# Summing the second layer's adaLN vectors on VectorE in pieces of 512 columns, from the first mixer on

## The chip, the core and the metric

The kernel runs on one core of a Trainium2 chip. Its engines are TensorE (PE, matrix products into PSUM), VectorE (DVE), ScalarE (ACT), GpSimd (POOL) and SyncE (SP, which issues most of the DMAs). The metric is the device time of one execution in microseconds (us), the median over runs. "Span" is the time from the first to the last instruction of the one execution that the profiler recorded.

## What is computed

Two layers over 256 tokens of width 2048. Each layer has a mixer and a channel mixer (ffn), each behind an RMSNorm that is modulated by vectors of an adaptive layer norm (adaLN), and each added back through a gate vector. The reference, cut to that:

```python
for layer in range(2):
    sh1, sc1, g1, sh2, sc2, g2 = split(silu(c) @ ada_w[layer] + ada_b[layer], 6)   # 6 vectors of 2048
    hn = rms_norm(h, norm_g[layer, 0]) * (1 + sc1) + sh1
    mix = even_mixer(hn, ...) if layer == 0 else chunk_mlp_mixer(hn, ...)
    h = h + g1 * mix
    hn2 = rms_norm(h, norm_g[layer, 1]) * (1 + sc2) + sh2
    h = h + g2 * conv_ffn(hn2, ...)
out = rms_norm(h, final_g)
```

`even_mixer` is a gated 31-tap convolution beside a state-space layer (S5), which also needs a projection of 256 context tokens; `chunk_mlp_mixer` (the odd mixer) is a gated MLP with a 128x128 mixing of tokens. Each adaLN vector (l, v) takes a matrix of 2048 x 2048 in f32, 16.8 MB, for one row of products. The six vectors of layer 1 together read about 100 MB.

## The kernel before

**Products.** Weights come in slabs of 128 x 2048 f32 (1 MB, tile `raw`, four buffers, `RAW`), by SP. A slab has two halves of 1024 columns; a half is split into `hi` (ScalarE, L129) and `lo` = raw - hi (L132, on VectorE, or on GpSimd for every `pool_every`-th half), three buffers each. A half feeds 12 matmuls of 512 columns: two token halves, two rows of the half, and three products each (L136 to L138: hi with xh, lo with xh, hi with xl). One half is called a half-step below. `groups` runs half-steps for one column group of a weight matrix, and after each of them gives some credit to queues of side work: `pump` (S5, convolution, LayerNorm pieces), `cpump`, and `ada_pump`.

**adaLN vectors.** `ada_q[0]` makes the vectors (0,2) to (0,5) on TensorE: a slab of `ada_w` in a `raw` buffer and four matmuls against `cst` (L199). `ada_q[1]` makes the six of layer 1 on VectorE, in the order (1,1), (1,0), (1,2), (1,4), (1,3), (1,5): for each of the 16 rows of slabs two slabs of 128 x 1024 (512 KB, tile `rawa`, two buffers in the pool `yp`), each with one product `acc = raw * cst[:, kt] + acc` (L241) into `adacc`, 128 x 2048. The bias row is loaded into partition 0 of a cleared `adacc` (a memset on GpSimd, L229, and a DMA, L230). At the end `fin` sums over the partitions with four matmuls of `ones` against `adacc`, side by side on 32 columns of the array each (L248), copies on ScalarE, and transposes on TensorE (vectors 0, 1, 3, 4) or writes a row to DRAM (`gate_out`, gates 2 and 5).

**Credits.** `ada_pump(n, k)` adds n credits to queue k and issues items while there is credit. A pair such as `(0.3, 0.48)` in `ADA_F0` gives queue 0 and queue 1 their credits for one slab, half of it after each half-step. Before, an item of queue 1 (one product of 1024 columns) costs 0.5. `ADA_F0` and `ADA_F1` belong to the ffn of layer 0 and 1 (first and second half of the input projection; output projection), `ADA_O1`, `ADA_O2` to the odd mixer's two projections. Before, queue 1 gets nothing in the even mixer. `ada_until` issues what is left of a vector when its consumer comes (`mod_vecs`, `gate_row`).

**Order.** The stages of the profiled execution, by time: the even mixer's first column groups up to 192 us; group 6 (24 matmuls a half-step, since the context is projected too) 192 to 260; groups 4 and 5, the S5 layer, the convolution and its LayerNorm 260 to 391; the even output projection 391 to 578; ffn of layer 0 578 to 1219 (input projection groups 629 to 799 and 896 to 1102, output projection 799 to 896 and 1102 to 1219); odd mixer 1219 to 1545; ffn of layer 1 1545 to 2118 in the same order (1603 to 1747 input, 1747 to 1846 output, 1846 to 2026 input, 2026 to 2118 output); final norm to 2130. The framework orders instructions on each engine by program order, with `high_priority` moving some ahead; each engine then works through its own queue in order.

Of the kernel before, what the change touches and what calls it, by code (L numbers as in the profile page):

```python
# [8 lines left out]
F32 = mybir.dt.float32  # L9
# [6 lines left out]
D = 2048  # L16
# [12 lines left out]
RC = {0: 3.0, 6: 2.5, 4: 2.5, 5: 2.5}  # L29
RS = {4: 2.0, 5: 2.0, 7: 0.4, 8: 2.2}  # L30
# [20 lines left out]
ADA_F0 = [((0.3, 0.48), (0.0, 0.44)), (0.0, 1.0)]  # L51
ADA_B = (0, 4, 0)
ADA_O1 = (0.0, 0.8)
ADA_O2 = (0.0, 0.7)
ADA_F1 = [((0.0, 0.54), (0.0, 0.5)), (0.0, 0.0)]
# [3 lines left out]
class Builder:  # L59
# [121 lines left out]
    def ada_setup(self, pe, dve):  # L181
        self.ada_q = [[i for lv in pe for i in self.ada_items(*lv)], [i for lv in dve for i in self.ada_items_v(*lv)]]
        self.ada_v = dve
        self.ada_credit = [0.0, 0.0]
        self.ada_T = {}
        self.ada_row = {}
# [35 lines left out]
    def ada_items_v(self, l, v):  # L222

        nc = self.nc
        st = {}

        def open_():
            acc = st["acc"] = self.yp.tile([128, D], F32, name="adacc", tag="adacc", bufs=1)
            nc.gpsimd.memset(acc, 0.0)  # L229
            nc.sync.dma_start(acc[0:1], self.A["ada_r"][l, v])  # L230

        def slab(i):
            kt, c = i // 2, slice(1024 * (i % 2), 1024 * (i % 2) + 1024)

            def f():
                if i == 0:
                    open_()
# [6 lines left out]
        def fin():  # L244
            acc = st["acc"]
            ps = self.ms_bank()
            for j in range(4):
                nc.tensor.matmul(ps[32 * j:32 * j + 32, :], self.ones[:, :32], acc[:, 512 * j:512 * j + 512],  # L248
                                 start=True, stop=True, tile_position=(0, 32 * j))
            x = self.small("wk", [128, 512], bufs=4)  # L250
            nc.scalar.activation(x, ps, AF.Copy)
            if v in (2, 5):
                self.gate_out(l, v, x)
                return
            tp = self.tp_bank()
            for b in range(4):
                nc.tensor.transpose(tp[:, 128 * b:128 * b + 128], x[:, 128 * b:128 * b + 128], self.ident)
            t = self.cp.tile([128, 1, 16], F32, name=f"adaT{l}{v}")
            nc.vector.tensor_copy(t[:, 0].rearrange("p (j b) -> p j b", j=4),
                                  tp.rearrange("p (b j r) -> p j b r", b=4, j=4)[:, :, :, 0])  # L260
            self.ada_T[l, v] = t

        return [(0.5, slab(k)) for k in range(2 * KT)] + [(0.5, lambda: None), (0.0, fin)]
# [166 lines left out]
    def setup(self):  # L430
# [6 lines left out]
        sil = self.small("sil", [128, 2, 16], bufs=1)  # L437
# [402 lines left out]
    def conv_setup(self, p):  # L840
# [6 lines left out]
        self.cvT = p.tile([32, 3 * NB + 128], F32, name="cvT")  # L847
# [5 lines left out]
    def conv31(self, m, z):  # L853
# [37 lines left out]
        def inv():  # L891
            ps = self.ms_bank()
            for b in range(2):
# [3 lines left out]
                nc.tensor.matmul(o, self.cvT[:, 3 * NB:], st["t"], start=False, stop=True)  # L897
# [6 lines left out]
    def even(self):  # L904
# [104 lines left out]
        for m in ORDER:  # L1009
            if m != 6:  # L1010
                gate(m, self.groups(W, [m], tok, q4, (ADA_E[m], 0.0), rate=RS[m], crate=RC[m])[m])
# [9 lines left out]
            ps = self.groups(W, [6], toks, [(q, 0) for q in range(4)], (ADA_E[6], 0.0), rate=0.0, crate=RC[6], width=4)[6]  # L1021
# [26 lines left out]
        while self.cv:  # L1048
            self.cpump(2.0)
            self.pump(RS[7])  # L1050
            self.ada_pump(ADA_C)
        mh, ml = self.mh, self.ml = self.xpair()
        for f in self.ln_items():
            f()
            self.pump(RS[7])
            self.ada_pump(ADA_C)
# [376 lines left out]
```

## Time and profile before

| | us |
|---|---|
| median of 3 runs | 2126.47 (2126.03 to 2138.9) |
| the profiled execution | 2132.22 |
| its span | 2130.4 |
| TensorE busy | 1969.8 |
| VectorE busy | 1589.1 |
| ScalarE busy | 963.5 |
| GpSimd busy | 770.1 |
| VectorE: products of the adaLN vectors (L241), 192 of them | 337.6 |

The profiler's views used here: the page of the whole execution; a table of busy time by stretch (also for one source line alone); groups of instructions by line; waits by who waited for whom; a timeline; DMA issues. Busy time of TensorE overlaps between neighbouring matmuls, so its share does not tell whether it runs at its peak; the length of a stretch that does the same work as another does.

### The profile page before, as it was taken

What the parts mean: (1) busy time and instruction counts of PE and PEld (TensorE: products, weight loads), DVE (VectorE), ACT (ScalarE), POOL (GpSimd) and SP (SyncE); (2) the same over time, 40 slices, a digit from 0 to 9 for tenths busy, and PEclk for the clock granted to TensorE, in tenths of its full rate; (3) what the DMA queues carried; (4) which work ended last, traced back from release to release, by engine and by line L of the source; (5) the groups of instructions that cost most, each with busy time, mean ns of one, the idle gap of its engine ahead of it and who ended that gap; (6) DMA issues with size and microseconds to landing.
All of it is one profiled execution on the core that took longest, in us unless ns stands there. A gap on an engine that the chain in (4) does not pass through costs nothing.

```text
span 2130.4 us, 25758 instructions
## 1 busy us (share of the span) xinstructions
PE 1969.8 (92%) x9412; PEld 1493.6 (70%) x9412; DVE 1589.1 (75%) x2535; ACT 963.5 (45%) x1323; POOL 770.1 (36%) x379
## 2 busy tenths in 40 slices
PE   5999999999799979999989799999899989999997
PEld 2566676667477747777777577777678867888886
DVE  5466376665679994879999776866778997368874
ACT  3354253743455433344444353343455544355553
POOL 4311143011034424444434244444434443444443
PEclk8999999999899999999999999999999999999999
DMA  9983553866886877876667778777766566555562
GB/s 375 401 345 109 185 193 142 328 262 219 305 306 225 295 299 254 294 269 230 217 243 267 266 271 292 251 254 274 273 230 215 198 242 238 182 191 185 183 203 108
DMA packets 91931, 522.90 MB, mean 245 GB/s; under 512 B 11318, under 2 KB 11750, under 8 KB 42262
## 3 DMA queue, kind: packets, MB, share of 16 engines
q1 hardware_dynamic: 88684, 517.09, 66.9%
q10 hardware_dynamic: 2736, 3.01, 0.4%
q8 instruction: 74, 1.21, 0.2%
q0 software_dynamic: 384, 1.16, 0.1%
q14 instruction: 53, 0.43, 0.1%
HBM read 519.09 MB, written 2.13 MB: 245 GB/s over the span
## 4 chain that ended last, share of the span: by engine, by line
PE 27%; DVE 15%; DMA 5%; issue 3%; ACT 1%; POOL 1%; ACTq 0%; SPq 0%; DVEq 0%; POOLq 0%
PE mm L137 9%; PE mm L138 9%; PE mm L136 8%; DVE adacc L241 5%; DMA rawa<-in_ada_w 5%; DVE lo L132 4%; DVE ca L1225 2%; DVE cg L1225 1%; POOL lo L132 1%; PE tp L1209 1%; ACT hi L129 0%; DVE al L1277 0%; DVE xl L399 0%; DMA lnrow<-in_o_ln 0%; DVE ca L1275 0%
## 5 line engine op out<-in xcount | busy, mean ns | idle before, releaser
L132 POOL TENSOR_TENSOR lo<-raw,hi 128x1024 fp32r<-128x1024 f32 x253 | 668.1, 2641 | 1208.5 <-ACT hi L129 1144.3
L129 ACT ACTIVATE hi<-raw 128x1024 fp32r<-128x1024 f32 x568 | 598.4, 1059 | 833.0 <-PE mm L138 659.0
L137 PE MATMUL mm<-lo,xh 128*128 128x512 f32 x1632 | 653.2, 400 | 44.8 <-DVE lo L132 44.7
L136 PE MATMUL mm<-hi,xh 128*128 128x512 f32 x1632 | 659.0, 405 | 0.9 <-ACT hi L129 0.6
L138 PE MATMUL mm<-hi,xl 128*128 128x512 f32 x1632 | 646.9, 397 | 1.7 <-DVE xl L399 1.2
L132 DVE TENSOR_TENSOR lo<-raw,hi 128x1024 fp32r<-128x1024 f32 x315 | 432.2, 1375 | 207.6 <-ACT hi L129 207.1
L241 DVE SCALAR_TENSOR_TENSOR adacc<-rawa,cst,adacc 128x1024 f32<-128x1024 f32 x192 | 337.6, 1766 | 92.2 <-DMA rawa<-in_ada_w 88.9
L137 PEld LDWEIGHTS mm<-lo,xh 128*128 128x128 f32 x1632 | 313.3, 192 | 120.2 <-DVE lo L132 58.8
L136 PEld LDWEIGHTS mm<-hi,xh 128*128 128x128 f32 x1632 | 311.7, 192 | 109.2 <-issue 31.1
L138 PEld LDWEIGHTS mm<-hi,xl 128*128 128x128 f32 x1632 | 312.6, 192 | 69.8 <-DVE xl L399 1.8
L137 PE MATMUL mm<-lo,ah 128*128 128x512 f32 x640 | 258.6, 404 | 12.4 <-DVE lo L132 11.6
L136 PE MATMUL mm<-hi,ah 128*128 128x512 f32 x640 | 257.5, 403 | 2.4 <-ACT hi L129 2.4
L138 PE MATMUL mm<-hi,al 128*128 128x512 f32 x640 | 257.1, 402 | 0.0
L1225 DVE SCALAR_TENSOR_TENSOR cg<-tp,fcw,cg 128x189 f32<-128x189 f32 (+2 forms) x512 | 180.7, 420 | 9.9 <-ACT cg L1212 9.9
L1225 DVE SCALAR_TENSOR_TENSOR ca<-tp,fcw,ca 128x189 f32<-128x189 f32 (+2 forms) x512 | 180.5, 419 | 9.7 <-ACT ca L1212 9.7
L137 PEld LDWEIGHTS mm<-lo,ah 128*128 128x128 f32 x640 | 122.7, 192 | 48.4 <-DVE lo L132 16.2
L136 PEld LDWEIGHTS mm<-hi,ah 128*128 128x128 f32 x640 | 122.3, 191 | 34.6 <-ACT hi L129 4.2
L138 PEld LDWEIGHTS mm<-hi,al 128*128 128x128 f32 x640 | 122.4, 191 | 30.6 <-issue 1.7
L199 PE MATMUL ad<-raw,cst 128*32 128x512 f32 x512 | 79.4, 614 | 6.9 <-DMA raw<-in_ada_w 6.9
L407 DVE TENSOR_TENSOR wk<-mm,grow 128x512 f32<-128x512 f32 x56 | 38.0, 684 | 27.8 <-PE mm L138 27.7
L408 DVE TENSOR_TENSOR h<-h,wk 128x512 f32<-128x512 f32 x56 | 56.8, 1022 | 1.2
L387 PE MATMUL tp<-ident,wk 128*128 128x128 f32 x160 | 28.3, 308 | 22.0 <-DVE wk L373 10.8
(273 smaller groups left out, 1462.8 us busy)
## 6 DMA issues: line engine op xcount, KB each, us to landing
raw<-in_f_w_in SPq DMA_DIRECT2D x128, 1024.0 KB, 4.9
rawa<-in_ada_w SPq DMA_DIRECT2D x192, 512.0 KB, 5.8
raw<-in_ada_w SPq DMA_DIRECT2D x84, 1024.0 KB, 5.2
raw<-in_f_w_out SPq DMA_DIRECT2D x64, 1024.0 KB, 4.9
raw<-in_o_w_in SPq DMA_DIRECT2D x32, 1024.0 KB, 5.3
raw<-in_e_w_in SPq DMA_DIRECT2D x28, 1024.0 KB, 6.7
raw<-in_e_w_out SPq DMA_DIRECT2D x16, 1024.0 KB, 5.2
raw<-in_o_w_out SPq DMA_DIRECT2D x16, 1024.0 KB, 5.4
```

Source lines behind the costliest of these rows:

```text
L129: nc.scalar.activation(hi, raw, AF.Copy)
L132: eng.tensor_sub(lo, raw, hi.bitcast(F32))
L136: nc.tensor.matmul(ps, xh, wh, start=first, stop=False)
L137: nc.tensor.matmul(ps, xh, wl, start=False, stop=False)
L138: nc.tensor.matmul(ps, xl, wh, start=False, stop=last)
L199: nc.tensor.matmul(st["ps"][32 * j:32 * j + 32, :], self.cst[:, kt], raw[:, 512 * j:512 * j + 512], start=kt == 0, stop=kt == KT - 1, tile ...
L241: nc.vector.scalar_tensor_tensor(a, raw, self.cst[:, kt, 0:1], a, op0=OP.mult, op1=OP.add)
L387: self.nc.tensor.transpose(tp[:, a * 256 + t * 128:a * 256 + t * 128 + 128], z[t][:, c0:c0 + 128], self.ident)
L407: nc.vector.tensor_mul(m, ps[t], row[:, c])
L408: nc.vector.tensor_add(h[:, t, c], h[:, t, c], m)
L1209: nc.tensor.transpose(tp[:, a * 256 + t * 128:a * 256 + t * 128 + 128], z[t][:, c0 + 128 * a:c0 + 128 * a + 128], self.ident)
L1225: nc.vector.scalar_tensor_tensor(oo, s[:, y0 + dy:y1 + dy, x0 + dx:x1 + dx], w, oo, op0=OP.mult, op1=OP.add)
```

## The change

The products of queue 1 are made for 512 columns at a time, and the queue gets credit from the first mixer on.

- A vector is four blocks j of 512 columns. A block clears an accumulator `adc` of 128 x 512 (in the pool `sp`, one buffer), loads its bias row, and then takes four slabs q of 1 MB from a re-laid-out copy `ada_x`, each with four products of 128 x 512. A product costs 0.25 credits, a slab and `fin` cost none.
- In the even mixer a slab lies in one of the weights' four `raw` buffers; from layer 0's ffn on (`self.late`) in `rawa`, two buffers of 1 MB.
- `fin(j)`: for shift and scale vectors four matmuls with 128 columns of `adc` as stationary operand against two columns of `ones`, and a copy of four columns on VectorE; for gates one matmul, a copy of 32 partitions on ScalarE, and a DMA of one row. It stands right behind the last product of its block.
- Credits: `ADA_V` is new for the even mixer, the credits of the two ffn and the odd mixer's input projection are lower.
- To make room: `sil` takes a `modr` buffer, and the convolution's bias row moves from the last row of `e_conv_w` to the first, so that the bias product uses one row of `ones` and `cvT` loses 128 columns.

```diff
+ADA_V = {6: 1.5, 4: 1.2, 5: 1.2, 7: 0.6, 8: 1.2, 9: 1.2}
-ADA_F0 = [((0.3, 0.48), (0.0, 0.44)), (0.0, 1.0)]
+ADA_F0 = [((0.3, 0.22), (0.0, 0.22)), (0.0, 0.8)]
-ADA_O1 = (0.0, 0.8)
+ADA_O1 = (0.0, 0.5)
 ADA_O2 = (0.0, 0.7)
-ADA_F1 = [((0.0, 0.54), (0.0, 0.5)), (0.0, 0.0)]
+ADA_F1 = [((0.0, 0.3), (0.0, 0.3)), (0.0, 0.0)]
...
     def ada_items_v(self, l, v):
...
-                raw = self.yp.tile([128, 1024], F32, name="rawa", tag="rawa", bufs=2)
-                nc.sync.dma_start(raw, self.A["ada_w"][l, v, kt, :, c])
-                a = st["acc"][:, c]
-                nc.vector.scalar_tensor_tensor(a, raw, self.cst[:, kt, 0:1], a, op0=OP.mult, op1=OP.add)
+        def slab(j, q):
+            def f():
+                if q == 0:
+                    st["acc"] = self.small("adc", [128, 512], bufs=1)
+                    nc.gpsimd.memset(st["acc"], 0.0)
+                    nc.sync.dma_start(st["acc"][0:1], self.A["ada_r"][l, v, :, 512 * j:512 * j + 512])
+                if self.late:
+                    raw = self.yp.tile([128, 4, 512], F32, name="rawa", tag="rawa", bufs=2)
+                else:
+                    raw = self.wp.tile([128, 2048], F32, name="raw", tag="raw", bufs=RAW)
+                    raw = raw.rearrange("p (k n) -> p k n", k=4)
+                nc.sync.dma_start(raw, self.A["ada_x"][l, v, j, q])
+                st["raw"] = raw
+            return f
+        def prod(j, q, k):
+            def f():
+                a = st["acc"]
+                kt = 4 * q + k
+                nc.vector.scalar_tensor_tensor(a, st["raw"][:, k], self.cst[:, kt, 0:1], a, op0=OP.mult, op1=OP.add)
+            return f
+        def fin(j):
+            def f():
+                acc = st["acc"]
+                ps = self.ms_bank()
+                if v in (2, 5):
+                    nc.tensor.matmul(ps[:32], self.ones[:, :32], acc, start=True, stop=True)
+                    x = self.small("wk", [128, 512], bufs=4)
+                    nc.scalar.activation(x[:32], ps[:32], AF.Copy)
+                    if j == 0:
+                        st["d"] = self.dp.tile([4, 512], F32, name="rowd", tag="rowd")
+                    nc.sync.dma_start(st["d"][j:j + 1], x[0:1])
+                    if j == 3:
+                        self.ada_row[l, v] = st["d"]
+                    return
+                for b in range(4):
+                    nc.tensor.matmul(ps[:, 2 * b:2 * b + 2], acc[:, 128 * b:128 * b + 128], self.ones[:, :2],
+                                     start=True, stop=True)
...
-        return [(0.5, slab(k)) for k in range(2 * KT)] + [(0.5, lambda: None), (0.0, fin)]
+        out = []
+        for j in range(4):
+            for q in range(4):
+                out.append((0.0, slab(j, q)))
+                out += [(0.25, prod(j, q, k)) for k in range(4)]
+            out += [(0.0, fin(j))]
+        return out
...
-                gate(m, self.groups(W, [m], tok, q4, (ADA_E[m], 0.0), rate=RS[m], crate=RC[m])[m])
+                gate(m, self.groups(W, [m], tok, q4, (ADA_E[m], ADA_V[m]), rate=RS[m], crate=RC[m])[m])
...
-            ps = self.groups(W, [6], toks, [(q, 0) for q in range(4)], (ADA_E[6], 0.0), rate=0.0, crate=RC[6], width=4)[6]
+            ps = self.groups(W, [6], toks, [(q, 0) for q in range(4)], (ADA_E[6], ADA_V[6]), rate=0.0, crate=RC[6], width=4)[6]
...
             self.ada_pump(ADA_C)
+            self.ada_pump(ADA_V[7], 1)
...
-        self.out_proj(WO, h, row, mh, ml, q4[:3], None, (ADA_EO, 0.0), rate=RS[8])
+        self.out_proj(WO, h, row, mh, ml, q4[:3], None, (ADA_EO, ADA_V[8]), rate=RS[8])
...
-        self.out_proj(WO, h, row, mh, ml, q4[3:], ssq, (ADA_EO, 0.0))
+        self.out_proj(WO, h, row, mh, ml, q4[3:], ssq, (ADA_EO, ADA_V[9]))
```

## Rows read from the trace of the kernel before

**Rows 1.** The page: busy time by engine; DMA rate in 40 slices of the span.

```profile
PE 1969.8 (92%) x9412; PEld 1493.6 (70%) x9412; DVE 1589.1 (75%) x2535; ACT 963.5 (45%) x1323; POOL 770.1 (36%) x379
...
GB/s 375 401 345 109 185 193 142 328 262 219 305 306 225 295 299 254 294 269 230 217 243 267 266 271 292 251 254 274 273 230 215 198 242 238 182 191 185 183 203 108
```

**Rows 2.** Stretches: length; busy PE, PEld, DVE, ACT, POOL; clock, DMA share, GB/s.

```profile
260.00:391.00 131.00, 125.30 (x921) 84.55 (x918) 88.21 (x158) 67.43 (x123) 46.22 (x56) 0.96 0.54 200
...
391.00:553.00 162.00, 154.28 (x964) 110.19 (x964) 104.35 (x175) 74.76 (x121) 16.87 (x7) 0.96 0.72 268
...
192.00:578.00 386.00, 359.63 (x2264) 246.34 (x2263) 236.25 (x417) 173.85 (x296) 70.95 (x66) 0.95 0.62 230
...
629.00:751.00 122.00, 121.46 (x574) 94.81 (x574) 115.09 (x218) 65.41 (x85) 54.39 (x21) 1.00 0.72 264
...
799.00:896.00 97.00, 94.25 (x392) 74.09 (x393) 59.90 (x50) 36.81 (x37) 45.86 (x18) 0.97 0.77 270
...
896.00:1102.00 206.00, 190.39 (x838) 152.86 (x837) 190.64 (x293) 95.20 (x120) 91.29 (x34) 0.98 0.68 242
...
1603.00:1747.00 144.00, 138.42 (x635) 113.09 (x634) 138.76 (x263) 78.19 (x101) 62.64 (x25) 1.00 0.60 213
...
1747.00:1846.00 99.00, 95.14 (x402) 74.36 (x401) 64.27 (x83) 39.26 (x42) 40.40 (x17) 0.98 0.61 217
...
1846.00:2026.00 180.00, 180.00 (x823) 149.11 (x822) 134.35 (x268) 95.68 (x119) 76.28 (x33) 1.00 0.54 187
...
2026.00:2118.00 92.00, 91.54 (x395) 73.18 (x393) 56.66 (x78) 40.81 (x52) 38.65 (x16) 1.00 0.44 149
```

**Rows 3.** The same stretches, line L241 alone: length, busy DVE, clock, DMA, GB/s.

```profile
629.00:751.00 122.00, 19.05 (x10) 1.00 0.72 264
...
799.00:896.00 97.00, 22.63 (x13) 0.97 0.77 270
...
896.00:1102.00 206.00, 59.54 (x31) 0.98 0.68 242
...
1603.00:1747.00 144.00, 22.87 (x11) 1.00 0.60 213
...
1747.00:1846.00 99.00, 13.82 (x8) 0.98 0.61 217
```

**Rows 4.** One stretch, line L199 alone: length, busy PE, busy PEld, clock, DMA, GB/s.

```profile
629.00:751.00 122.00, 6.39 (x48) 0.95 (x48) 1.00 0.72 264
```

**Rows 5.** Groups by line: busy us, mean ns | idle before; last: 192 to 578.

```profile
L241 DVE SCALAR_TENSOR_TENSOR adacc<-rawa,cst,adacc 128x1024 f32<-128x1024 f32 x192 | 337.6, 1766 | 92.2 <-DMA rawa<-in_ada_w 88.9 <-DMA adacc<-in_ada_r 2.9
...
L407 DVE TENSOR_TENSOR wk<-mm,grow 128x512 f32<-128x512 f32 x56 | 38.0, 684 | 27.8 <-PE mm L138 27.7
...
L408 DVE TENSOR_TENSOR h<-h,wk 128x512 f32<-128x512 f32 x56 | 56.8, 1022 | 1.2
...
L248 PE MATMUL ms<-adacc,ones 128*32 128x512 f32 x48 | 9.5, 605 | 5.9 <-DVE adacc L241 5.8
...
L387 PE MATMUL tp<-ident,wk 128*128 128x128 f32 x160 | 28.3, 308 | 22.0 <-DVE wk L373 10.8 <-ACT modr L396 8.2 <-DVE ada0T L492 3.0
...
L241 DVE SCALAR_TENSOR_TENSOR adacc<-rawa,cst,adacc 128x1024 f32<-128x1024 f32 x5 | 6.4, 1279 | 0.0
```

**Rows 6.** Waits, whole span: who waited for what, us, times, longest.

```profile
PE mm L137 <- DVE lo L132: 56.3, 39, 2.9
...
DVE adacc L241 <- DMA rawa<-in_ada_w: 88.9, 41, 5.5
```

**Rows 7.** Waits of PE from 391 to 529 us.

```profile
PE mm L137 <- DVE lo L132: 3.7, 3, 2.7
```

**Rows 8.** Timeline in layer 0's ffn: start, us, engine; idle before in brackets.

```profile
898.98 0.49 PE L137 MATMUL mm<-lo,xh 128*128 128x512 f32 x1 [2.50 <-DVE lo L132]
...
901.06 0.63 PE L138 MATMUL mm<-hi,xl 128*128 128x512 f32 x1
```

**Rows 9.** DMA issues: times, KB each, median us to landing.

```profile
rawa<-in_ada_w SPq DMA_DIRECT2D x192, 512.0 KB, 5.8
```

More of the change, by code (lines that the diff above doesn't have):

```diff
@@ L184, in ada_setup @@
         self.ada_credit = [0.0, 0.0]
+        self.late = False
         self.ada_T = {}
@@ L225, in ada_items_v @@
         st = {}
[L227 to L233, printed above, removed]
-            def f():
-                if i == 0:
-                    open_()
-                raw = self.yp.tile([128, 1024], F32, name="rawa", tag="rawa", bufs=2)
-                nc.sync.dma_start(raw, self.A["ada_w"][l, v, kt, :, c])
-                a = st["acc"][:, c]
-                nc.vector.scalar_tensor_tensor(a, raw, self.cst[:, kt, 0:1], a, op0=OP.mult, op1=OP.add)
-            return f
@@ L244, in fin @@
[L244 to L261, printed above, removed]
@@ new lines, in prod @@
+        def prod(j, q, k):
[21 more added lines that the diff above has]
+                                     start=True, stop=True)
+                if j == 0:
+                    st["t"] = self.cp.tile([128, 1, 16], F32, name=f"adaT{l}{v}")
+                nc.vector.tensor_copy(st["t"][:, 0, 4 * j:4 * j + 4],
+                                      ps[:, :8].rearrange("p (b r) -> p b r", r=2)[:, :, 0])
+                if j == 3:
+                    self.ada_T[l, v] = st["t"]
+            return f
@@ L436, in setup @@
         nc.gpsimd.memset(self.ones, 1.0)
-        sil = self.small("sil", [128, 2, 16], bufs=1)
+        sil = self.small("modr", [128, 256])[:, :32].rearrange("p (s k) -> p s k", s=2)
         nc.scalar.activation(sil, self.cT, AF.Silu)
@@ L896, in inv @@
                     nc.tensor.matmul(o, self.cvG[:, part], st["p", b][:, part], start=part == 0, stop=False)
-                nc.tensor.matmul(o, self.cvT[:, 3 * NB:], st["t"], start=False, stop=True)
+                nc.tensor.matmul(o, self.ones[0:1], st["t"][0:1], start=False, stop=True)
             nc.scalar.activation(self.z2[:, :, c], ps.rearrange("p (b n) -> p b n", b=2), AF.Copy)
@@ L1056, in even @@
             self.ada_pump(ADA_C)
+            self.ada_pump(ADA_V[7], 1)
         zcp.__exit__(None, None, None)
@@ L1303, in program @@
         self.yp = self.ctx.enter_context(self.tc.tile_pool(name="yp", bufs=1))
+        self.late = True
         if stop == 2:
@@ L1368, in layout @@
     ang = np.arange(31)[:, None] * om
[L1369 to L1371 removed]
+    t = np.zeros((32, 3 * NB), np.float32)
+    t[1:] = np.concatenate([np.cos(ang), -np.sin(ang), np.sin(ang)], 1)
     A["cv_t"] = t
```

8 lines of the change are left out of this document (3 added, 5 removed).

## The prediction, made before the changed kernel was run

> **What bounds the kernel now.** I read the page first. TensorE is busy for 92% of the span, VectorE for 75% [rows 1]. The page warns that matmuls overlap, so 92% does not say that TensorE runs at its peak. The table by stretch says it, because the two ffns do the same work. In layer 1 the last eight column groups of the input projection (1846 to 2026) take 180 us, with TensorE busy throughout and its clock fully granted; no adaLN product runs there. Layer 0's same eight groups (896 to 1102) take 206 us with a clock of 0.98 [rows 2] and hold 31 adaLN products, 59.5 us of VectorE [rows 3]. So a column group costs 180/8 = 22.5 us when TensorE is the bound, and the second layer's adaLN work costs TensorE time where it lies.
>
> How it does so is in the waits. TensorE waits 56 us in 39 pieces for `lo` halves that VectorE is late with, and VectorE itself stands 89 us in 41 pieces before an adaLN product whose slab has not landed, with the `lo` halves queued behind it [rows 6]. The slab takes 5.8 us to land [rows 9]. The timeline shows one such stall: 2.5 us idle before the matmul of L137, and two us later matmuls that take 0.63 us where the first behind the stall took 0.49 [rows 8]; the granted clock of that stretch is 0.98, not 1.00 [rows 2], so part of it ran at the lower level of 1.2 GHz, which adds to the stall.
>
> The even mixer is different. From 192 to 578 us TensorE is busy 360 of 386 us, VectorE 236, GpSimd only 71 [rows 2]; in its output projection TensorE waits for VectorE's `lo` for just 3.7 us [rows 7]. VectorE has 150 us free there. That is the place the change fills.
>
> **The change, part by part.**
>
> *How much moves.* One credit is four products of 512 columns, one slab of 1 MB, two of the old products. The even mixer gets: group 6, 8 half-steps of 0.75, 6 credits; groups 4 and 5, 8 of 0.6 each, 9.6; the convolution's and LayerNorm's 13 items of 0.6, 7.8; the output projection's first part 19 half-steps of 0.6 (6 for each of three groups, 1 in the last because of `HOLD`), 11.4; its second part 6 of 0.6, 3.6. Together 38.4 of 96 credits, 154 new products, as many columns as 77 old ones. Later remain 57.6 credits, the columns of 115 old products. Before, 5 of the 192 ran before 578 us [rows 5], 187 later. So the later part loses 72. The consumers' due times are kept: 72 credits by the end of layer 0's ffn cover (1,0), (1,1) and more, and the queue is empty early in layer 1's ffn, where before the last products ran until the output projection.
>
> *What a late product costs.* Four stretches against their twins without products [rows 2, 3]: 206 - 180 = 26 us for 31 products; 144 - 135 (six groups of 22.5) = 9 for 11; 97 - 92 = 5 for 13; 99 - 92 = 7 for 8. Together 47 us for 63 products: 0.75 us each, from 0.38 to 0.88. Removing 72 gives -54 us.
>
> *What the narrower product costs.* The trace has no product of 512 columns. The nearest rows on VectorE are 684 ns (L407, one input in PSUM) and 1022 ns (L408, both inputs in SBUF, its mean over quiet and contended stretches) [rows 5]. The old product takes 1279 ns in the even mixer, where GpSimd is mostly idle, and 1766 over all [rows 5]. I take 0.69 us in the even mixer: a pair takes 1.38 us for 1.28, 8% more. For the 115 later that is 115 x 0.75 x 0.08 = +7 us; bounds are nothing and 16% (two of 1022 against 1766), +14. On this the Trainium skill speaks against the change: "VectorE: DVE Perf Modes", the section on the TRN2 errata, says each VectorE instruction pays a fixed time, and that many small tiles pay it each; by its formula for a two-input f32 operation the pair would cost 0.157 us more than the single one, an estimate of 30 us of VectorE over all 192 pairs. The rows above give 0.10 us, 19 us of VectorE; by the skill's figure the sum would be some 4 us worse.
>
> *Slab waits.* VectorE waited 0.46 us per old product for slabs (89 of 192) [rows 6], 21% of the time these products held it. A new slab serves twice the columns and is asked for when the last one's products are done, a few half-steps ahead. I halve that part: 115 x 0.75 x 0.21 / 2 = -9; bounds 0 and -18.
>
> *More closings.* There are 24 `fin` instead of 6, each directly behind its last product, without the old empty item between. TensorE waited 5.8 us for L241 at six closings [rows 5], 0.97 each; behind the waiting matmul stand all other matmuls, and on GpSimd the next block's memset waits for it with `lo` halves behind. 15 later ones instead of 6: +9; 9 in the even mixer: +9. Their own work: 64 small matmuls for the four shift and scale vectors, each below the 308 ns of the transposes on 128 columns (L387), and 8 of 605 ns for the gates, against 48 of L248 that lie four deep (9.5 us) and 16 transposes [rows 5]. That is between -10 and +10 us; I take 0. SP issues 96 slabs fewer and 24 small DMAs more, GpSimd clears the same bytes: nothing, beneath SP's waits for free buffers. `sil` and the bias row: one activation at the start, 24 matmuls with the same columns; nothing.
>
> *What 154 products cost in the even mixer.* 154 x 0.684 = 105 us, in 150 us of free VectorE [rows 2]: 90% busy. It is tightest from 260 to 391, with 17.4 credits, 70 products or 48 us, against 43 free. From below: nothing, if all of it fits. From above: 0.75 to 0.88 us per old product, as later. Between them stands 629 to 751: VectorE is 115 of 122 us busy, with the clock fully granted [rows 2]. Five groups at 22.5 are 112.5, TensorE's own adaLN matmuls 6.4 [rows 4], so 3 us are lost over 19 us of products [rows 3]: 0.16 per us of VectorE. A nearly full VectorE is no loss if its inputs are there. I take this row, since in the even mixer too half-steps are long, `lo` is three buffers ahead, and GpSimd is out of the way: 105 x 0.16 = +17.
>
> *DMA.* The output projection (391 to 553) moves 268 GB/s [rows 2]; 15 slabs in 162 us make it 365. The page's third slice reached 401 [rows 1], so it fits: 0. "DMA: Bandwidth & Descriptors" of the Trainium skill gives some 358 GB/s of HBM for one core in its specifications; an estimate by it is 3 us more, and the row of 401 speaks against that limit here.
>
> **Sum**: later -54 + 7 - 9 + 9 = -47; even mixer 17 + 9 = +26; together -21 us. The span of 2130.4 becomes 2109. The median of the runs, 2126.5, lies 4 us below the profiled span; minus 21 it is 2105.
>
> **Rivals.**
>
> *The even mixer pays as the ffn does.* A slab there holds one of the four `raw` buffers from its issue until its fourth product, and SP's next weight slab stands behind it; VectorE is overfull from 260 to 391; a late S5 piece stops TensorE in its order. Then each of the 77 costs the highest late price: 77 x 0.88 = 68, with the closings 77, minus 47: +30, 2156. It is no longer faster from (47 - 9)/77 = 0.49 us per old product, slower by 1% from 0.77. For it: 43 us free against 48 asked. Against it: rows 7, and GpSimd's idleness.
>
> *The late losses are not the products'.* If the stalls come mostly from `lo` contending with GpSimd, and fewer products thin them only at the lowest price, 0.38: -27 + 4 - 5 + 9 = -19, plus 26: +7, 2133. The change then moves work without a gain. For it: the output projections, 5 us for 13 products.
>
> *The even mixer is free.* All 154 products lie in idle VectorE, only closings cost, and the late price is 0.88: -63 + 8 - 11 + 9 = -57, plus 9: -48, 2078. For it: 150 free us, and the fewer blocked `lo` halves.
>
> **Chances.** Forecast 0.45, its own range 2078 to 2133; even mixer dear 0.20; late price low 0.18; even mixer free 0.17. One per cent is 21 us, about what a measurement of this kernel can tell from no change. Faster by more: all of the last and half of the first, 0.42. Within: the rest of the first, the low price and a little of the dear case, 0.40. Slower: 0.18. The range 2074 to 2146 leaves out most of the dear case and the far end of the free one.
>
> **What would show it.** Right: 896 to 1102's eight groups at 185 to 195 us, layer 1's first six at 136, waits of TensorE for `lo` halved; the even mixer (up to layer 0's ffn) some 25 us later than 578, new products at about 0.69 us there. Wrong: the ffn starting beyond 610 us or before 585, `hi` or `lo` waiting for weight slabs before 578, long waits of TensorE at the closings, or layer 0's eight groups still above 200 us.

## The result: 4.3% slower, and the profile after

The changed kernel takes 2223.09 us (median of 4 runs) against 2131.47 us of the kernel before on the same chip: a ratio of 1.0428, interval 1.0388 to 1.0468. The prediction was 2105 us, 2074 to 2146. In the profiled executions the span grew from 2130.4 to 2221.8 us. First the page: no engine's busy time changed by more than 5% [rows 1]; what is new is the row of TensorE's clock, with dips from the sixth to the 13th slice (278 to 722 us) and single ones behind; the kernel before has an 8 only in its first and 11th slice.

```profile
PE 2004.1 (90%) x9492; PEld 1525.2 (69%) x9492; DVE 1600.8 (72%) x2739; ACT 964.8 (43%) x1325; POOL 730.7 (33%) x397
...
PEclk8999989779898999899999989999989999999999
...
GB/s 391 380 335 130 229 206 209 273 258 302 283 324 241 265 214 230 280 273 278 224 210 192 238 253 245 188 239 248 260 231 175 188 180 183 189 189 189 180 199 114
```

The stages, each from the first matmul of its first column group. "Late" is everything from layer 0's ffn to the end.

| us | even mixer from group 6 | layer 0's ffn starts | late | span |
|---|---|---|---|---|
| before | 386.1 | 578.3 | 1552.1 | 2130.4 |
| after | 494.3 | 692.8 | 1529.0 | 2221.8 |

So the late part gained 23 us, where -47 was forecast, and everything up to layer 0's ffn lost 115, where +26 was forecast. Of the 115, 6 lie ahead of group 6; over all runs of this study group 6 starts between 190 and 199 us, so the length of the stage, 108 us more, is the safer figure. The table by stretch of the changed kernel (length; busy PE, PEld, DVE, ACT, POOL; clock, DMA share, GB/s) shows the same: first the even mixer from group 6, whole and in five parts, then three stretches of layer 0's ffn and one of layer 1's.

```profile
198.50:692.80 494.30, 397.90 (x2334) 270.47 (x2333) 341.81 (x574) 174.81 (x297) 70.03 (x75) 0.86 0.69 258
...
198.00:271.00 73.00, 68.58 (x332) 45.40 (x332) 40.39 (x65) 24.34 (x42) 9.06 (x8) 1.00 0.54 196
271.00:333.00 62.00, 54.82 (x424) 40.86 (x425) 45.54 (x66) 25.99 (x51) 21.07 (x29) 0.86 0.59 221
333.00:466.00 133.00, 97.28 (x578) 64.78 (x577) 105.42 (x197) 51.82 (x91) 19.51 (x28) 0.80 0.70 261
466.00:631.00 165.00, 135.75 (x824) 95.17 (x823) 110.45 (x174) 53.37 (x81) 15.95 (x8) 0.87 0.71 269
...
631.00:693.00 62.00, 42.19 (x183) 24.64 (x182) 40.56 (x78) 19.30 (x35) 4.45 (x3) 0.83 0.86 332
...
909.40:1019.60 110.20, 98.35 (x394) 77.50 (x395) 76.70 (x76) 36.60 (x36) 44.72 (x19) 0.92 0.69 256
1019.60:1207.60 188.00, 183.94 (x842) 151.04 (x841) 173.46 (x298) 95.10 (x119) 86.92 (x35) 1.00 0.63 230
1207.60:1336.40 128.80, 106.33 (x425) 83.57 (x423) 102.56 (x151) 46.62 (x61) 43.67 (x20) 0.88 0.64 237
...
1709.10:1846.70 137.60, 137.60 (x634) 113.44 (x633) 118.30 (x259) 78.25 (x101) 57.78 (x25) 1.00 0.52 184
```

The reader is to see three things. The late input projections came out as forecast: layer 0's last eight groups take 188 us (before 206), layer 1's first six 137.6 (before 144). Layer 0's output projections grew from 97 and 117 us to 110 and 129, at a clock of 0.92 and 0.88; they hold 38 and 42 narrow products, the columns of 19 and 21 old ones, where 13 and 23 old ones stood. And in the even mixer VectorE is busy for 342 of 494 us, so it has as much idle time as before, 152 us, while TensorE's granted clock fell from 0.95 [rows 2] to 0.86.

The groups from 198 to 693 us (busy us, mean ns | idle before and its releasers) and the waits of the same stretch, of the engines first, then of SP's queue:

```profile
L249 DVE SCALAR_TENSOR_TENSOR adc<-raw,cst,adc 128x512 f32<-128x512 f32 x148 | 114.4, 773 | 26.2 <-DMA raw<-in_ada_x 12.5 <-DMA adc<-in_ada_r 12.3
L130 ACT ACTIVATE hi<-raw 128x1024 fp32r<-128x1024 f32 x56 | 56.6, 1050 | 70.3 <-DMA raw<-in_e_w_out 40.8 <-DMA raw<-in_e_w_in 14.9 <-PE mm L139 12.7
...
L234 POOL MEMSET adc<- 128x512 f32 x10 | 5.2, 524 | 210.8 <-PE ms L267 152.6 <-PE ms L257 58.1
```

```profile
POOL adc L234 <- PE ms L267: 152.6, 7, 32.7
...
ACT hi L130 <- DMA raw<-in_e_w_out: 40.8, 7, 10.6
...
PE mm L138 <- DVE lo L133: 28.9, 9, 7.7
...
PE mm L137 <- ACT hi L130: 23.1, 9, 4.3
...
PE ms L267 <- issue: 10.0, 1, 10.0
PE ad L201 <- DMA raw<-in_ada_w: 9.5, 4, 8.4
...
SPq L235 <- POOL adc L234: 48.8, 8, 9.0
```

Read in the program's order, these waits form a ring. A closing (L267) stands on TensorE until the block's last product; the next block's memset (L234) waits for it; the bias row (L235) waits for the memset on SP, up to 9.0 us, with weight slabs behind it in SP's queue; and a weight slab that comes late holds up `hi` (40.8 us; before, 4.8 us in 4 pieces), then `lo` and TensorE. The timeline from 449 to 467 us has it in one place (start, us, engine; idle before in brackets):

```profile
449.59 0.33 SPq L157 DMA_DIRECT2D raw<-in_e_w_out  x1
...
451.63 1.86 PE L201 MATMUL ad<-raw,cst 128*32 128x512 f32 x8
...
457.00 2.00 ACT L130 ACTIVATE hi<-raw 128x1024 fp32r<-128x1024 f32 x2 [7.33 <-DMA raw<-in_e_w_out]
...
462.65 0.74 DVE L249 SCALAR_TENSOR_TENSOR adc<-raw,cst,adc 128x512 f32<-128x512 f32 x1
...
463.50 1.84 PE L267 MATMUL ms<-ones,adc 128*128 128x2 f32 x8 [10.01 <-issue]
465.38 0.16 DVE L271 COPY adaT<-ms 128x4 f32<-128x4 f32 x1 [1.64 <-PE ms L267]
465.40 0.53 POOL L234 MEMSET adc<- 128x512 f32 x1 [31.09 <-PE ms L267]
...
465.95 0.25 SPq L235 DMA_DIRECT2D adc<-in_ada_r  x1
466.25 0.33 SPq L241 DMA_DIRECT2D raw<-in_ada_x  x1
466.63 0.76 SPq L157 DMA_DIRECT2D raw<-in_e_w_out  x1
```

TensorE is idle for 10 us until the last product of the block (462.65) is done; the profile names no releaser for this wait, but the matmul reads what that product writes, and it starts 0.1 us behind it. The memset, the bias row, the next slab and the next weight slab then go out one behind the other. The `hi` halves had been ready since 459, but their matmuls stand behind L267 in TensorE's order.

A second place, 594 to 606 us, shows what such a stop does behind itself:

```profile
594.88 2.01 ACT L130 ACTIVATE hi<-raw 128x1024 fp32r<-128x1024 f32 x2 [6.41 <-DMA raw<-in_e_w_out]
...
596.30 0.39 PE L138 MATMUL mm<-lo,xh 128*128 128x512 f32 x1
...
600.80 3.10 DVE L249 SCALAR_TENSOR_TENSOR adc<-raw,cst,adc 128x512 f32<-128x512 f32 x4
...
603.82 1.22 DVE L133 TENSOR_TENSOR lo<-raw,hi 128x1024 fp32r<-128x1024 f32 x1
...
605.09 0.79 PE L138 MATMUL mm<-lo,xh 128*128 128x512 f32 x1 [7.72 <-DVE lo L133]
```

The weight slab came 6.4 us late, `lo` then stood behind four products, TensorE stopped for 7.7 us, and the matmul that took 0.39 us before takes 0.79 after the stop. Summed over the trace's clock records, TensorE ran at the 1.2 GHz level for 134 us between group 6 and layer 0's ffn, before for 37; the pauses of more than 1.8 us from one matmul's start to the next sum to 88 us, before 20.

### The profile page after: what moved, and what is told of

Its sections match the earlier page's. It is cut to its first block, busy times and chain, and to the rows that moved or that the text cites. A ratio compares the mean times of both kernels' runs of the same rounds, so it can differ in the third digit from the quotient of the medians.

```text
span 2221.8 us, 25996 instructions
## 1 busy us (share of the span) xinstructions
PE 2004.1 (90%) x9492; PEld 1525.2 (69%) x9492; DVE 1600.8 (72%) x2739; ACT 964.8 (43%) x1325; POOL 730.7 (33%) x397
## 4 chain that ended last, share of the span: by engine, by line
PE 66%; DVE 18%; issue 6%; DMA 5%; ACT 3%; POOL 2%; ACTq 0%; SPq 0%; DVEq 0%; POOLq 0%
PE mm L138 19%; PE mm L139 18%; PE mm L137 18%; DVE adc L249 6%; DVE lo L133 4%; PE ad L201 2%; POOL lo L133 2%; DMA raw<-in_ada_w 1%; DMA rawa<-in_ada_x 1%; DVE ca L1247 1%; PE tp L1231 1%; DMA raw<-in_e_w_in 1%; ACT hi L130 1%; DVE h L428 1%; DVE w L786 1%
## 5 line engine op out<-in xcount | busy, mean ns | idle before, releaser
L133 POOL TENSOR_TENSOR lo<-raw,hi 128x1024 fp32r<-128x1024 f32 x253 | 634.0, 2506 | 1123.0 <-ACT hi L130 1042.1
L133 DVE TENSOR_TENSOR lo<-raw,hi 128x1024 fp32r<-128x1024 f32 x315 | 403.6, 1288 | 286.0 <-ACT hi L130 285.9
L249 DVE SCALAR_TENSOR_TENSOR adc<-rawa,cst,adc 128x512 f32<-128x512 f32 x228 | 251.3, 1102 | 14.4 <-DMA adc<-in_ada_r 5.6
L249 DVE SCALAR_TENSOR_TENSOR adc<-raw,cst,adc 128x512 f32<-128x512 f32 x156 | 120.3, 771 | 26.3 <-DMA raw<-in_ada_x 12.5
L234 POOL MEMSET adc<- 128x512 f32 x24 | 12.6, 526 | 259.9 <-PE ms L267 180.2
```

The costliest lines, as they stand in the source:

```text
L133: eng.tensor_sub(lo, raw, hi.bitcast(F32))
L249: nc.vector.scalar_tensor_tensor(a, st["raw"][:, k], self.cst[:, kt, 0:1], a, op0=OP.mult, op1=OP.add)
```

## Experiments

Each kernel was run and profiled once; only the last was timed more often (10 executions). All are edits of the changed kernel unless it is said otherwise. The table has their stages, as above. How far single executions can be compared: the kernel before took 2120 to 2139 us over all its executions; the even mixer, where nothing of it was edited (before, e10_form, e14_formboth, e15_formhalf), takes 380 to 386 us; the late part, where it is the changed kernel's (after, e1, e2, e4, e5, e7, e13), takes 1529 to 1539. So a difference of less than about 10 us in one run is not told from chance.

| us | even mixer from group 6 | layer 0's ffn starts | late | span |
|---|---|---|---|---|
| after | 494.3 | 692.8 | 1529.0 | 2221.8 |
| e1_small | 483.8 | 680.2 | 1532.4 | 2212.6 |
| e2_noslab | 421.3 | 620.4 | 1532.2 | 2152.6 |
| e3_biaspool | 481.9 | 676.8 | 1547.5 | 2224.3 |
| e4_noopen | 459.1 | 654.6 | 1532.8 | 2187.4 |
| e5_tinyslab | 421.8 | 613.9 | 1539.0 | 2152.9 |
| e6_burst | 465.8 | 658.6 | 1539.3 | 2197.9 |
| e7_noslab_noopen | 397.0 | 595.3 | 1530.6 | 2125.9 |
| e8_biasend | 468.9 | 665.8 | 1527.3 | 2193.1 |
| e9_latefin | 465.6 | 660.9 | 1539.0 | 2200.0 |
| e10_form | 382.1 | 576.7 | 1617.4 | 2194.1 |
| e11_m6 | 396.8 | 591.6 | 1608.7 | 2200.3 |
| e12_best | 390.1 | 585.8 | 1582.3 | 2168.0 |
| e13_slabonly | 428.5 | 621.9 | 1529.0 | 2150.9 |
| e14_formboth | 382.7 | 577.4 | 1600.6 | 2178.0 |
| e15_formhalf | 380.1 | 575.3 | 1617.2 | 2192.5 |
| e16_bnoopen | 381.7 | 572.0 | 1543.9 | 2115.9 |

### Is it VectorE, or the slabs? e1_small, e2_noslab, e5_tinyslab

```diff
# e1_small: products of 16 columns in the even mixer
+n = 512 if self.late else 16
-nc.vector.scalar_tensor_tensor(a, st["raw"][:, k], ...)
+nc.vector.scalar_tensor_tensor(a[:, :n], st["raw"][:, k, :n], ...)
# e2_noslab: no slab there, products of full width read the constant cst
+else: st["raw"] = None; return
# e5_tinyslab: as e1_small, and a slab brings 64 of its 2048 columns
+nc.sync.dma_start(raw[:, :64], ...[:, :64])
```

> In the even mixer each product takes 16 columns instead of 512 (the other 496 are left out, so those adaLN vectors are incomplete); slabs, openings and closings stay. Takes VectorE's 120 us of products there away. If VectorE's load is the cause: layer 0's ffn starts near 600 us instead of 693, total near 2130. If slabs in the weights' buffers or SP's waits are the cause: start stays above 660, total above 2190.

> In the even mixer no slab is loaded and the products read a constant tile of the same size (so those vectors are not the weights' sums); products, openings and closings stay. If the slabs are the cause (a raw buffer held, 39 MB more to move, SP's queue): ffn start near 600 us, total near 2130. If VectorE's load or the openings are: start above 660, total above 2190.

> As e1_small, but the even mixer's slab loads bring 64 of 2048 columns (the rest of these vectors is left out): the raw buffers are taken and SP's queue is used as before, the bytes and DMA time are gone. If the bytes are what the slabs cost: ffn start near 600 us (e1_small 680). If it is the buffers held or the order on SP: start above 650.

Measured, by the start of layer 0's ffn: e1_small 680.2 us, 13 less than the changed kernel; e2_noslab 620.4, 72 less; e5_tinyslab 613.9, 66 less than e1_small. The even mixer's row of e1_small and of e5_tinyslab:

```profile
196.40:680.20 483.80, 395.77 (x2334) 268.32 (x2333) 269.93 (x574) 174.73 (x296) 71.72 (x75) 0.87 0.69 264
```

```profile
192.10:613.90 421.80, 371.32 (x2334) 254.39 (x2333) 267.08 (x573) 173.76 (x297) 72.63 (x75) 0.93 0.59 214
```

VectorE's load is not the cause: in e1_small it falls from 342 to 270 us and the stretch only by 10.5. The slabs are. e5_tinyslab keeps their buffers and SP's order, and a slab holds its buffer, from its issue to its fourth product, for 14.1 us on average against 16.3; the buffers held at once are 1.24 of four in both. Only the bytes are gone (the columns of 37 slabs, 37.6 of 127.7 MB, in the same 18714 packets), and with them 66 us, 62 of the stage, at mean rates below what the first slices of the page reach (264 and 214 against 380 to 391 GB/s). In the even mixer TensorE waits for the halves like this, first in e1_small, then in e5_tinyslab:

```profile
PE mm L137 <- ACT hi L130: 31.9, 9, 10.8
PE mm L138 <- DVE lo L133: 18.7, 7, 6.1
...
PE mm L137 <- ACT hi L130: 12.4, 7, 3.5
PE mm L138 <- DVE lo L133: 10.3, 8, 3.5
```

That is 50.6 us against 22.7; the changed kernel has 52.0, e2_noslab 3.7, the kernel before 4.6. ScalarE's own waits for weight slabs are no measure of the loss: 32 us in e1_small and 54 in e5_tinyslab, which is the faster one.

### The openings: e3_biaspool, e4_noopen, e8_biasend

```diff
# e3_biaspool: the bias row from GpSimd's queue
-nc.sync.dma_start(st["acc"][0:1], ...)
+nc.gpsimd.dma_start(st["acc"][0:1], ...)
# e4_noopen: in the even mixer no memset and no bias row; the first product writes adc
+nc.vector.tensor_scalar(a, st["raw"][:, k], self.cst[:, kt, 0:1], None, op0=OP.mult)
# e8_biasend: so everywhere, and the bias is added when the block closes
-nc.vector.tensor_copy(st["t"][:, 0, 4*j:4*j+4], ps...)
+nc.vector.tensor_add(st["t"][:, 0, 4*j:4*j+4], ps..., st["t"][:, 0, 4*j:4*j+4])
```

e4_noopen leaves out the bias of the vectors made in the even mixer; e8_biasend computes everything.

> The bias row of every block is loaded from GpSimd's queue instead of SP's, so SP no longer stands behind the memset that waits for the closing matmuls (56 us in 8 waits from 271 to 631 us in the changed kernel). If SP's standing is the cause: ffn start near 620 us and late stages 10 to 20 us shorter, total 2120 to 2150. If not: start within 10 us of 693, total 2205 to 2230.

> In the even mixer a block has no memset and no bias row: its first product writes the accumulator (so the bias is left out of those vectors). Openings are gone from GpSimd and SP; the first product itself must still wait for the closing matmuls. If openings as a whole are the cause: ffn start near 620. If only SP's standing counts, the same as with the bias row on GpSimd's queue, within 10 us. If neither: start near 690.

> The full computation, with no opening in any block: the first product writes the accumulator, and the bias is added at the closing. If openings cost as e4 showed for the even mixer: ffn start near 655. If they also cost in the later stages (24 memsets that wait for closings, with halves of weights behind them on GpSimd): the later part is 10 to 25 us shorter than the changed kernel's 1529 us; if not, the same within 5.

The ffn starts 16, 38 and 27 us earlier than in the changed kernel (the stage is 12, 35 and 25 us shorter). So SP standing behind the bias row may be part of it, but e3_biaspool's late part is 18 us longer, where 10 to 20 less were expected, and its whole time, 2226.11 us, is no better than the changed kernel's. The ring through the memset is more, and a computation that is whole and has no opening at all gains 27 us. In e8_biasend the late part doesn't answer to openings (1527.3 against 1529.0 us).

### The closings and the order of products: e9_latefin, e6_burst

```diff
# e9_latefin: an empty item of half a credit ahead of a closing, as before the change
-out += [(0.0, fin(j))]
+out += [(0.5, lambda: None), (0.0, fin(j))]
# e6_burst: a slab costs 1 credit, its four products follow at once
-out.append((0.0, slab(j, q))); out += [(0.25, prod(j, q, k)) for k in range(4)]
+out.append((1.0, slab(j, q))); out += [(0.0, prod(j, q, k)) for k in range(4)]
```

> An empty item of 0.5 credits stands before every closing, as the kernel before had it, so a closing comes one or two half-steps behind its last product. In the changed kernel four closings in layer 0's output projections stopped TensorE 4.2 to 4.6 us each, with the lower clock behind it. If that is what eats the later gain: the part from layer 0's ffn on is 15 to 30 us shorter than 1529, total near 2195. If products or slabs do it: within 5 of 1529.

> A slab now costs one credit and its four products nothing, so they are issued together and the slab's buffer comes free right after its landing (in the changed kernel a slab holds its raw buffer for 19 us on the mean, 1.4 of the 4 buffers). Same bytes, products, openings. If the holding is the cause: ffn start 30 us or more before 693. If bytes or the order of SP's queue: within 10 us of 693.

The ffn starts 32 us earlier with the closings put off, and 34 earlier with the products together (the stage is 29 us shorter in each). Neither run changes one thing alone. In e9_latefin the empty items use up credits, so 33 slabs lie in the even mixer and not 37; at 1.2 to 1.8 us a slab (below), 5 to 7 us of its gain are an estimate of that. In e6_burst a slab still holds its buffer for 15.9 us, against 19.2 in the changed kernel, so the buffer hardly comes free sooner, and its gain doesn't show that the holding is the cause, as its expectation would have it. The late part of e9_latefin is 10 us longer, where 15 to 30 less were expected: what the empty items left over is issued at layer 1's first output projection, whose first half takes 62.6 us, against 45.7. Of layer 0's output projections the second takes 119 us instead of 129, with closings that stop TensorE for 0.5 us instead of 10.7; the first takes 110 as in the changed kernel, and two closings still stop TensorE there for 11.5 us.

### What is left, and the slabs by themselves: e7_noslab_noopen, e13_slabonly

```diff
# e7_noslab_noopen: e2_noslab and e4_noopen together
# e13_slabonly: in the even mixer the 1 MB slabs and four products of 16 columns each, no opening, no closing matmul
```

e7_noslab_noopen leaves out the slabs' data and the bias, e13_slabonly the vectors that belong to the even mixer's credits.

> Even mixer without slabs (products read a constant tile) and without memset and bias rows (both left out of those vectors); products and closings stay. If slabs (-72 us) and openings (-38 us) are two separate causes that together are the whole loss: ffn start 580 to 595. If they are one and the same wait: start near 620 as without slabs alone. VectorE's load and closings are then what is left over 578.

> In the even mixer only the slabs of 1 MB remain of the second layer's adaLN work, each read by four products of 16 columns so that its buffer comes free as before; no accumulator is cleared, no bias row loaded and no closing matmul issued there, and those vectors are left out of the computation. From layer 0's ffn on it is the changed kernel. Theory that the slabs' bytes cost by themselves: what they made between the run with full slabs and the run with 64 columns of each, 66 us, is added to the kernel before, so layer 0's ffn starts at 578 + 66 = about 644 us. Rival, that the slabs only cost together with openings and closings (each lets a late weight slab meet a stopped TensorE): the ffn starts below 600 us. In either case what follows the even mixer takes 1525 to 1540 us.

e7_noslab_noopen has all 154 products at full width and all closings there, and its ffn starts at 595.3 us, 17 later than before the change. Slabs and openings together are therefore 97 of the 108 us by which the stage grew. Its even mixer:

```profile
198.30:595.30 397.00, 366.22 (x2334) 251.62 (x2333) 330.94 (x565) 175.52 (x298) 75.95 (x66) 0.95 0.60 224
```

VectorE busy for 331 of 397 us, and the clock 0.95 as before. With slabs alone (e13_slabonly) the ffn starts at 621.9, 44 later than before the change and between the two expectations. So the slabs cost by themselves, 44/37 = 1.2 us each, and beside openings and closings some 66/37 = 1.8. Its row: 296 GB/s over the whole stretch, `hi` waits 39.5 us in 6 pieces for output weights as in the changed kernel, and TensorE 32.7 us for the halves.

```profile
193.00:622.00 429.00, 367.33 (x2267) 248.22 (x2266) 264.25 (x574) 172.42 (x295) 72.08 (x66) 0.93 0.78 296
```

### The later part: e10_form, e14_formboth, e15_formhalf

```diff
# e10_form: the new form with the credits of before, nothing in the even mixer
+ADA_V = {6: 0, 4: 0, 5: 0, 7: 0, 8: 0, 9: 0}; ADA_F0, ADA_O1, ADA_F1 as before
# e14_formboth: e10_form with the edits of e8_biasend and e9_latefin
# e15_formhalf: e10_form with slabs of 512 KB and two products, four buffers
-rawa [128, 4, 512], bufs=2
+rawa [128, 2, 512], bufs=4
```

> The new form of the products with no credit in the even mixer and with the credits of the kernel before in the later stages: only the form is changed. If the form is as cheap as was forecast (7 us narrower products, 9 us slab waits less, 9 to 18 us closings): total 2130 to 2150. If closings cost 4 to 6 us each: 2180 to 2230. The even mixer must be as before (ffn start 578 to 585) if nothing but the credits there matters.

> The new form with the credits of before (nothing of the second layer's vectors in the even mixer), without openings (the first product of a block writes the accumulator, the bias is added at the closing) and with an empty item of 0.5 ahead of each closing; the whole computation. With openings and closings the form alone took 1617 us from layer 0's ffn to the end, 65 more than before. Theory that openings and closings make that loss: 1555 to 1570 us, the time of one execution 2130 to 2145. Rival, that the narrower products make it (384 of them hold VectorE for 426 us against 338 for the 192 wide ones): 1590 to 1605 us, 2170 to 2185.

> The new form with the credits of before, openings and closings as in the change, but slabs of 512 KB with two products each in four buffers, in place of 1 MB with four products in two. The bytes held are the same. Theory that slabs of 1 MB late in the kernel delay weight slabs behind them: 1580 to 1600 us from layer 0's ffn to the end, against 1617 with 1 MB slabs. Rival, that it is the products' number and the blocks' openings and closings: 1610 to 1625 us.

The form alone lengthens the late part from 1552.1 to 1617.4 us, +65, and leaves the even mixer as it was. Openings gone and closings put off give 17 of it back (1600.6); smaller slabs give nothing (1617.2). By the expectation of e14_formboth the other 48 us would be the narrow products', but its trace shows something else first. TensorE's waits at closings, first in e10_form, then in e14_formboth:

```profile
PE ms L267 <- DVE adc L249: 24.0, 6, 10.3
PE ms L257 <- DVE adc L249: 23.4, 6, 11.6
...
PE ms L267 <- issue: 10.8, 4, 3.6
```

```profile
PE ms L263 <- DVE adc L255: 19.9, 4, 6.4
PE ms L274 <- DVE adc L255: 19.1, 6, 6.1
...
PE ms L274 <- DVE rnr L370: 11.0, 1, 11.0
```

That is 58 us in 16 waits, 2.4 for each of the 24 closings, where the kernel before has 5.8 in two, and still 50 us in 11 with the closings put off: half a credit doesn't put them off far enough. TensorE's late waits for `lo` fell meanwhile from 50 us (before) to 25 (e10_form). So closings are where the form costs TensorE its time. Whether their products are late because they are narrower and more, or because the closing stands so close behind them, no run separates. The products over the whole span of e10_form:

```profile
L249 DVE SCALAR_TENSOR_TENSOR adc<-rawa,cst,adc 128x512 f32<-128x512 f32 x380 | 426.0, 1121 | 15.1 <-DMA adc<-in_ada_r 8.4 <-DMA rawa<-in_ada_x 0.9 <-issue 0.7
```

A pair takes 2.24 us, where one old product took 1.77 [rows 5]: 27% more, 88 us of VectorE over the kernel. VectorE's waits for late slabs, 88.9 us before [rows 6], are 0.9 here, and the late part grew all the same. From e10_form to the changed kernel the late part falls by 88 us for the work of 72 old products that moved out of it, 1.2 us each.

### Looking for a faster version: e11_m6, e12_best, e16_bnoopen

```diff
# e11_m6: e10_form, and 1.5 credits in group 6 alone
# e12_best: e11_m6 with the edits of e8_biasend and e9_latefin; the whole computation
# e16_bnoopen: the kernel before, its first products write adacc, the bias is added at the closing
-nc.gpsimd.memset(acc, 0.0)
-nc.sync.dma_start(acc[0:1], self.A["ada_r"][l, v])
+nc.vector.tensor_scalar(a, raw, self.cst[:, kt, 0:1], None, op0=OP.mult)   # kt == 0
-nc.scalar.activation(x, ps, AF.Copy)
+nc.sync.dma_start(x, self.A["ada_b"][l, v]); nc.vector.tensor_add(x, ps, x)
```

> As e10_form, and 1.5 credits a slab in column group 6 alone (192 to 260 us, where the DMA engines are 46% busy and VectorE 28 of 68 us): 6 slabs and 24 products early. If bytes beside a busy DMA are what costs in the even mixer, these 6 are nearly free: ffn start within 10 us of e10_form's, total 5 us less than e10_form or equal. If any slab costs 1.8 us there (66 us for 37): start 10 us later or more.

> The full computation. e11_m6 with closings put off by an empty item and with no openings (the first product writes the accumulator, the bias comes in at the closing). If openings and closings are what the form costs: 10 to 60 us less than e11_m6 and near 2125. If the narrow products cost: like e11_m6.

> The kernel before with its six openings taken away: the first product of a half writes the accumulator, and the bias is added on VectorE at the closing; the whole computation. VectorE waited 2.9 us for bias rows in the kernel before, and six memsets of 128 x 2048 go from GpSimd. If openings cost there what they cost in the changed kernel's even mixer (38 us for some 10 of them), the time falls by 10 to 20 us; if they only cost where TensorE's closings and weight slabs stand close, it stays within 6 us of the kernel before.

Six credits in group 6 (e11_m6), the quietest place, cost 15 us there and bring 9 late, the latter no more than chance can make. The fastest whole computation in the new form (e12_best) has an even mixer 4 us longer than before, which is within chance, and is still 38 us of span slower: the form's price in the later part remains. e16_bnoopen is a little faster than the kernel before: 2122.23 us against 2131.69, ratio 0.9966 (interval 0.9945 to 0.9988), some seven us, between its two expectations. It takes the one good part of this study, an accumulator that needs no opening, and leaves the wide products; it also moves the closing's copy from ScalarE to VectorE, so the gain isn't shown to be the openings' alone.

## Why the prediction was wrong, step by step

**What bounds the kernel.** Right for the ffns: layer 0's eight groups were forecast at 185 to 195 us and took 188, layer 1's six at 136 and took 137.6; TensorE's late waits for `lo` fell from 50 to 25 us, the half that was forecast. But three of the prediction's four signs of being wrong came too: the ffn started at 693 us, beyond 610, `hi` waited for weight slabs, and TensorE stood long at closings.

**"DMA: 0, for it fits".** This is the step that failed most. The bytes of 37 slabs cost 66 us in the changed kernel and 44 by themselves. The step compared a mean rate with the best slice. But a slab is not needed at a mean rate: SP issues the next weight slab only when a buffer is free, `hi` waits for it, and each 1 MB ahead of it can make it later. The trace before had a hint of it: in the even mixer an adaLN or weight slab landed 4.9 to 5.9 us after its issue (medians), and `hi` already waited for weights for 23 us there. The specifications of "DMA: Bandwidth & Descriptors" in the Trainium skill give some 358 GB/s: the even mixer's mean of 258 GB/s stayed far below it, and of the stretches above only 631 to 693 us (332) came near. Single slices of 12 us reached 416, and 421 before the change, so neither this figure nor the row of 401 was a lid there. The medians of the weight slabs' landing hardly moved (4.9 and 5.8 us, before 5.2 and 5.9). Whether the DMA engines were full for moments, or the slabs only stood in the wrong order, isn't shown; in e13_slabonly they are at least 90% busy in 14 of the stage's 40 slices, in the changed kernel in 5, before in 4.

**Openings "nothing, beneath SP's waits".** 38 us in the even mixer (e4_noopen). That SP waits anyway doesn't hide a small transfer that waits for another engine: everything behind it in the queue goes out later.

**Closings at 0.97 us.** The price was taken from six closings that had an empty item between them and their last product [rows 5]. Directly behind it, one closing stopped TensorE for 10 us in the even mixer, and putting all of them off, with four slabs fewer, gave 32 us there. Late, six closings stopped TensorE for 26.0 us, against 5.8 in the whole kernel before. Four of these waits in layer 0's output projections, of about 4 us each:

```profile
963.91 1.05 PE L257 MATMUL ms<-adc,ones 128*32 128x512 f32 x2 [3.80 <-DVE adc L249]
...
1000.72 1.87 PE L267 MATMUL ms<-ones,adc 128*128 128x2 f32 x8 [4.00 <-DVE adc L249]
...
1245.97 1.87 PE L267 MATMUL ms<-ones,adc 128*128 128x2 f32 x8 [3.78 <-DVE adc L249]
...
1284.70 1.84 PE L267 MATMUL ms<-ones,adc 128*128 128x2 f32 x8 [4.21 <-issue]
```

**Products in the even mixer at +17.** No failure: without slabs and openings, but with the closings, they cost 17 us by the ffn's start and 11 by the stage (e7_noslab_noopen), where products and closings were forecast at 26, and their width changes 13 and 10.5 (e1_small). At 0.77 us each instead of 0.684 they left VectorE idle for 152 us. (236 and 105 of 386 us are 88%, not the 90% stated.)

**The later part, -47.** It was -23, of two unlike halves. The input projections of both ffns and of the odd mixer, with layer 1's first output projection, became 54 us shorter for the work of 83 old products less in them: 0.66 us each, near the 0.75 of the forecast. The two output projections of layer 0's ffn and the odd mixer's became 31 us longer (13, 12 and 7), with the columns of 64 old products in them instead of 57. All six late waits at closings lie in these three, so the term that failed here is the closings: forecast at 0.97 us each, they stop TensorE for 26.0 us, and the clock of layer 0's two is 0.92 and 0.88. The terms for the form were off as a whole: over all 192 pairs they give +14, and the form alone costs +65 (e10_form), with 52 us more of TensorE's waits at closings. The narrower product was taken at 8% over the old one; it is 27% over all products. What the fixed cost of an instruction does was understated too. By the formula of "VectorE: DVE Perf Modes" of the Trainium skill (its section on the TRN2 errata) a pair takes an estimated 0.157 us more; I used 0.10, and the trace has 2 x 0.773 - 1.279 = 0.27 in the even mixer and 0.48 over e10_form, so the Trainium skill's warning was right and its figure too low here.

**The rivals.** The nearest was "the even mixer pays as the ffn does": it had the right place and the right sign, but 77 us with its closings against a measured 115. Its mechanism holds only in part. VectorE was not overfull (e1_small, e7_noslab_noopen), and a stop of TensorE by a late product is there, but at closings; TensorE does wait for halves of late weight slabs, but for the bytes ahead of them more than for buffers held (e5_tinyslab, which keeps the buffers and is 62 us shorter). "The late losses are not the products'" had the late part at -19, near the measured -23, but by luck: it took the low price of 0.38 us per product, and where products left and no closing stopped TensorE, the price was 0.66.

**What stays open.** The parts in the even mixer don't add up: 66 for bytes, 38 for openings, 32 for closings and 13 for width are more than 115. That a late weight slab costs most where TensorE already stands would explain it, and slabs alone cost less than slabs beside openings and closings (44 against 66), but no run shows the closings' share by itself. The slower clock belongs to it: 69 us more in pauses, and 97 us more at the 1.2 GHz level, half of which, 49, is an estimate of the time that level costs (a matmul of 0.39 us takes 0.79 there). No run held the clock, so this split isn't shown. In the later part it stays open why the products before a closing are late.

## What to carry to other kernels

When side work is moved beside a stage with few buffers, cost its transfers by what stands behind them in the queue and in the buffers, not by a mean rate; ask of each small transfer, memset and closing matmul which engine it waits for and what waits behind it. Splitting an operation is paid at its duration in the stage where it runs, not at the quietest one in the trace. And "there is idle time on that engine" is a statement about one engine: here it was true, and the stage still became 28% longer (494 against 386 us).

## What the runs showed of the hardware that was not expected

Pauses are paid twice. Across the even mixer TensorE's pauses grew from 20 to 88 us, and the granted clock fell from 0.95 to 0.86, with 1.2 GHz for 134 us instead of 37; a 128x512 matmul took 0.39 us ahead of a pause of 7.7 us and 0.79 behind it. And a 512-column product of two SBUF operands took 773 ns in the changed kernel's even mixer, with GpSimd busy for 14% of it, and 1121 ns over the whole of e10_form, a ratio of 1.45, where the 1024-column product went from 1279 (five of them) to 1766, 1.38 [rows 5]; that GpSimd's work makes the difference is not shown.
